# Two of eight pairs of contraction tiles in gate and up as seven products of mixed tiles in place of eight

## Chip, cores and metric

One core of a Trainium2 chip. The metric is device time in microseconds (us) of one execution, as a median of runs; the kernel before took 2430.54 us (three runs, 2429.72 to 2430.84). Durations inside the kernel come from one profiled execution.

## What is computed

A two-layer decoder trunk in fp32 over 256 tokens of width 2048: a Mamba-2 layer, then a layer of sliding-window attention, each followed by a dense SwiGLU feed-forward block, with RMSNorm around every part. The change touches the feed-forward block of both layers only:

```
D_MODEL = 2048
SEQ = 256
D_FF = -(-8 * D_MODEL // (3 * 256)) * 256      # 5632

def swiglu(u, w_gate, w_up, w_down):
    return (jax.nn.silu(u @ w_gate) * (u @ w_up)) @ w_down

for layer in range(DEPTH):
    ...
    ffn = swiglu(rmsnorm(h, g[2]), ffn_w_gate[layer], ffn_w_up[layer], ffn_w_down[layer])
    h = h + rmsnorm(ffn, g[3])
```

## The kernel before

**Tiles.** The tokens lie transposed, 16 contraction tiles (kt) of 128 features by 256 tokens; the 256 tokens are two token tiles (t) of 128. The 5632 hidden columns are worked in 11 units of 512 (`u`). In a unit, gate runs over the 16 contraction tiles for both token tiles (`a_form`, L277), then up does. The products accumulate in PSUM, one bank of 128 x 512 for each token tile; there are eight banks in all (L154).

**Three products for one.** Every fp32 number is held as a sum of a high and a low part of type fp32r. A product of two numbers is three matmuls (`a_mm`, L291): high by high, high by low, low by high (L298, L299, L300). So one token tile, one contraction tile and 512 columns cost three matmuls, and a pair of contraction tiles of gate and up for both token tiles costs 2 x 2 x 2 x 3 = 24.

**Weights.** The class `Weights` (L33) holds a list of weight tiles in the order in which they are used. A tile is two contraction tiles by 512 columns, 512 KB, loaded by SP into one of five `raw` buffers (`_load`, L54). It is then split by `_convert` (L62): ScalarE copies it to `whi` (L78), VectorE subtracts `whi` from it into `wlo` (L79); of each there are four buffers. `next` (L85) is called when TensorE's products of a tile are written down: it lets conversion run up to three tiles ahead and loads up to four ahead of that. So a tile can be converted when the tile four places earlier has had its last product, and a raw buffer can be loaded again when the tile in it is converted.

**A unit's end.** When gate is complete, ScalarE takes the Silu of both banks into `scr` (L576). When up is complete, VectorE multiplies the two banks by the row factor `rs` and by the Silu (L579). Two weight tiles into the next unit, `store` (L558) transposes the result by TensorE (eight transposes of 128 x 128, L563) and splits it into `hh` and `hl` (L186, L187), which are the input of the down products (`mix_stage`, L425). Such late steps are put on a list `todo` and called by a hook after each weight tile.

**Unit 0** differs: its gate products are interleaved with the norm and the transposes that make the tokens' tiles `xx` (`a_first`, L484).

Each engine works its instructions in the order in which they were put down; SP's queue issues the loads in the order of the list.

Of the kernel before, what the change touches and what calls it, by code (L numbers as in the profile page):

```python
# [22 lines left out]
KF = FF // P  # L23
EPS = 1e-6
NH = 64
CW = 512
HW = CW // 2
SUB = 2
RAWB = 5
CVB = 4  # L30


class Weights:  # L33

    def __init__(self, nc, pool, specs, scaled, raw_ahead=RAWB - 1, cv_ahead=CVB - 1):
        self.nc, self.pool, self.specs, self.scaled = nc, pool, specs, scaled
        self.raw_ahead, self.cv_ahead = raw_ahead, cv_ahead  # L40
        self.subs, self.first = [], {}
        for i, (key, ap) in enumerate(specs):
            a = ap.shape[1]
            n = ap.shape[2]
            per = (SUB * CW) // n
            for s in range(0, a, per):
                self.first.setdefault(key, len(self.subs))
                self.subs.append((i, s, per, n, key))
        self.raw = []
        self.cv = []  # L50
        self.pin = lambda ins: ins
        self.pos = 0

    def _load(self, upto):  # L54
        while len(self.raw) < min(upto, len(self.specs)):
            key, ap = self.specs[len(self.raw)]
            _, a, n = ap.shape
            t = self.pool.tile([P, a, n], F32, tag="raw", name="raw", bufs=RAWB)
            self.nc.sync.dma_start(t[:], ap)
            self.raw.append(t)  # L60

    def _convert(self, upto):  # L62
        nc = self.nc
        while len(self.cv) < min(upto, len(self.subs)):
            i, s, per, n, key = self.subs[len(self.cv)]
            self._load(i + 1)
            src = self.raw[i][:, s : s + per, :]
            hi = self.pool.tile([P, per, n], F32R, tag="whi", name="whi", bufs=CVB)
            lo = self.pool.tile([P, per, n], F32R, tag="wlo", name="wlo", bufs=CVB)
            if key in self.scaled:  # L70
                k0 = per * (len(self.cv) - self.first[key])
                for k in range(per):
                    f = self.scaled[key][:, k0 + k : k0 + k + 1]
                    nc.scalar.activation(hi[:, k, :], src[:, k, :], AF.Copy, scale=f)
                    nc.vector.scalar_tensor_tensor(lo[:, k, :], src[:, k, :], f, hi[:, k, :].bitcast(F32),
                                                   ALU.mult, ALU.subtract)
            else:
                self.pin(nc.scalar.copy(hi[:], src))  # L78
                self.pin(nc.vector.tensor_tensor(lo[:], src, hi[:].bitcast(F32), ALU.subtract))  # L79
            self.cv.append((hi, lo))  # L80
# [18 lines left out]
def tile_yoco(ctx: ExitStack, tc: tile.TileContext, a: dict):  # L99
    nc = tc.nc  # L100
# [9 lines left out]
    scaled = {}  # L110

    def add(key, w, kts, n0, nn=CW):
        nk = SUB * CW // nn
        for k in range(0, kts, nk):
            specs.append((key, wap(w, k, nk, n0, nn)))
# [18 lines left out]
        add("wout%d" % c, a["ssm_w_out"][0], DI // P, CW * c)  # L134

    def add_ffn(l):
        for u in range(FF // CW):
            add("gate%d_%d" % (l, u), a["ffn_w_gate"][l], KD, CW * u)
            add("up%d_%d" % (l, u), a["ffn_w_up"][l], KD, CW * u)
        for c in range(4):  # L140
            add("down%d_%d" % (l, c), a["ffn_w_down"][l], KF, CW * c)

# [37 lines left out]
    def new_xt(pool=xtpool):  # L180

        xx = pool.tile([P, KD, 2, T], F32R, tag="xx", name="xx")
        return xx[:, :, 0, :], xx[:, :, 1, :], xx

    def split_bank(dh, dl, src):
        nc.scalar.copy(dh, src)  # L186
        nc.vector.tensor_tensor(dl, src, dh.bitcast(F32), ALU.subtract)  # L187
# [116 lines left out]
    xt = new_xt()  # L304
# [99 lines left out]
    first = (xr, rr0, first_unit, first_squares, first_rstd, first_row, renorm)  # L404
# [119 lines left out]
    def row_factor():  # L524

        return [norm_stats(hpool, h, t) for t in range(NT)]
# [12 lines left out]
    def by_row(o, src, rr):  # L539

        nc.vector.tensor_tensor(o.rearrange("p (c t) -> p c t", c=2), src.rearrange("p (c t) -> p c t", c=2),
                                rr[:].unsqueeze(1).broadcast_to([P, 2, T]), ALU.mult)

    def ffn(layer, mix):
        xt = new_xt()
        with tc.tile_pool(name="ffn%d" % layer, bufs=1, side="right") as fp:
            hh = fp.tile([P, KF, T], F32R, tag="hh", name="hh")
            hl = fp.tile([P, KF, T], F32R, tag="hl", name="hl")
            scr = hpool.tile([P, 2 * NT, CW], F32, tag="gpost", name="scr")
            todo = []  # L550

            def hook():
                if todo:
                    f = todo.pop(0)
                    if f is not None:
                        f()

            def store(u):  # L558

                for t in range(NT):  # L560
                    pt = bank()
                    for k in range(4):
                        nc.tensor.transpose(pt[:, P * k : P * (k + 1)], scr[:, NT + t, P * k : P * (k + 1)], ident[:])  # L563
                    split_bank(hh[:, 4 * u : 4 * u + 4, P * t : P * (t + 1)],
                               hl[:, 4 * u : 4 * u + 4, P * t : P * (t + 1)],
                               pt[:].rearrange("p (k t) -> p k t", k=4))

            rs = None
            for u in range(FF // CW):
                if u == 0:  # L570
                    gb = a_first("gate%d_%d" % (layer, u), mix, gt[:, layer, 2, :], xt)
                    rs = row_factor()
                else:
                    gb = a_form("gate%d_%d" % (layer, u), xt, KD, hook=hook)
                for t in range(NT):
                    nc.scalar.activation(scr[:, t, :], gb[t][:], AF.Silu, scale=rs[t][:, 0:1])  # L576
                ub = a_form("up%d_%d" % (layer, u), xt, KD, hook=hook)
                for t in range(NT):
                    nc.vector.scalar_tensor_tensor(scr[:, NT + t, :], ub[t][:], rs[t][:, 0:1], scr[:, t, :],  # L579
                                                   ALU.mult, ALU.mult)  # L580
                todo += [None, lambda u=u: store(u)]
            return mix_stage("down%d_" % layer, (hh, hl), KF, layer, 3, hook=hook, lag=2 if layer == 0 else CVB)


    mix = mix_stage("wout", (yh, yl), DI // P, 0, 1, bk0=bk0)
# [497 lines left out]
```

## Time and profile before

| what | value |
|---|---|
| median of three runs | 2430.54 us |
| the profiled execution | 2430.55 us, span 2428.8 us |
| granted TensorE clock | 0.999 |
| TensorE busy | 2409.6 us, 99% of the span, 11810 matmuls |
| VectorE busy | 1461.5 us, 60% |
| ScalarE busy | 1221.8 us, 50% |
| matmuls of gate, up and the shared k and v by a_mm, each of L298, L299, L300 | 1440 |
| HBM read | 449.56 MB, 186 GB/s over the span |

The profile gives for every engine the time in which it was busy, for every group of instructions a count and a mean length, and for idle time the instruction that ended it. TensorE's matmuls overlap each other in the pipeline, so their lengths (about 390 ns) are not what one costs: the distance from start to start is. For VectorE and ScalarE the length of a group's instruction is near its cost, a little over it where one follows another.

Loads of 512 KB are issued on SP's queue, and the profile gives the time from issue to landing.

### The profile page before, as it was taken

How to read it: one execution, taken by the hardware profiler on the slowest of the kernel's cores; microseconds unless marked ns; L12 is line 12 of the kernel's file. 1: busy time of each engine (PE TensorE's matmuls, PEld its weight loads, DVE VectorE, ACT ScalarE, POOL GpSimd, SP SyncE). 2: the span in 40 equal slices, each digit the busy share in tenths (PEclk: the TensorE clock that was granted, in tenths of full speed). 3: DMA queues.
4: the chain of work that ended last, by engine and by line, in shares of the span. 5: the costliest groups of instructions: out<-in, count | busy, mean ns of one | idle time of the engine just before them, and what ended most of it. 6: DMA issues, size and time to landing. Idle time of an engine off the chain costs nothing.

```text
span 2428.8 us, 30963 instructions
## 1 busy us (share of the span) xinstructions
PE 2409.6 (99%) x11810; PEld 2001.9 (82%) x11810; DVE 1461.5 (60%) x2017; ACT 1221.8 (50%) x1721; POOL 84.2 (3%) x66
## 2 busy tenths in 40 slices
PE   9999999999999999999999999999999999999998
PEld 8888888888878888888888878777888888888887
DVE  6998878874465445445444468866545455454444
ACT  6566866654454444444444467755444444444443
POOL 2500100000000000000000000000000000000000
PEclk9999999999999999999999999999999999999999
DMA  7666666657656666666666664345666666666664
GB/s 221 183 204 190 189 189 187 178 183 249 191 169 193 185 191 191 189 190 191 205 192 194 194 187 156 127 127 154 204 190 187 191 191 190 190 190 207 193 193 145
DMA packets 284404, 453.75 MB, mean 187 GB/s; under 512 B 16976, under 2 KB 115536, under 8 KB 283488
## 3 DMA queue, kind: packets, MB, share of 16 engines
q1 hardware_dynamic: 283936, 451.39, 62.1%
q8 instruction: 92, 1.51, 0.3%
q14 instruction: 56, 0.46, 0.1%
q10 hardware_dynamic: 288, 0.33, 0.0%
q0 software_dynamic: 32, 0.07, 0.0%
HBM read 449.56 MB, written 2.16 MB: 186 GB/s over the span
## 4 chain that ended last, share of the span: by engine, by line
PE 97%; ACT 1%; DVE 1%; issue 0%; POOL 0%; DVEq 0%; POOLq 0%; ACTq 0%
PE bank L299 23%; PE bank L300 23%; PE bank L298 23%; PE bank L240 14%; PE bank L245 7%; PE bank L563 1%; PE bank L785 1%; PE bank L961 1%; PE bank L1004 1%; PE bank L360 1%; ACT xx L219 0%; PE bank L996 0%; ACT whi L78 0%; ACT junk L202 0%; PE bank L770 0%; PE bank L788 0%
## 5 line engine op out<-in xcount | busy, mean ns | idle before, releaser
L79 DVE TENSOR_TENSOR wlo<-raw,whi 128x1024 fp32r<-128x1024 f32 x785 | 960.0, 1224 | 867.0 <-ACT whi L78 866.5
L78 ACT CAST whi<-raw 128x1024 fp32r<-128x1024 f32 x785 | 826.4, 1053 | 997.3 <-PE bank L300 911.4
L298 PE MATMUL bank<-whi,xx 128*128 128x512 f32 x1440 | 562.7, 391 | 2.5 <-ACT xx L219 2.1
L300 PE MATMUL bank<-whi,xx 128*128 128x512 f32 x1440 | 561.3, 390 | 0.9 <-DVE xx L220 0.9
L299 PE MATMUL bank<-wlo,xx 128*128 128x512 f32 x1440 | 561.1, 390 | 0.5 <-DVE wlo L79 0.5
L240 PE MATMUL bank<-xx,whi 128*128 128x512 f32 (+1 forms) x1488 | 523.9, 397 | 0.0
L245 PE MATMUL bank<-xx,wlo 128*128 128x256 f32 (+1 forms) x1488 | 416.7, 285 | 0.0
L240 PEld LDWEIGHTS bank<-xx,whi 128*128 128x128 f32 (+1 forms) x1488 | 277.0, 188 | 61.2 <-issue 0.4
L298 PEld LDWEIGHTS bank<-whi,xx 128*128 128x128 f32 x1440 | 270.4, 188 | 60.2 <-ACT xx L219 4.2
L300 PEld LDWEIGHTS bank<-whi,xx 128*128 128x128 f32 x1440 | 270.4, 188 | 58.9 <-DVE xx L220 2.8
L299 PEld LDWEIGHTS bank<-wlo,xx 128*128 128x128 f32 x1440 | 270.5, 188 | 56.3 <-DVE wlo L79 1.4
L245 PEld LDWEIGHTS bank<-xx,wlo 128*128 128x128 f32 (+1 forms) x1488 | 280.5, 189 | 11.3 <-issue 7.0
L298 PE MATMUL bank<-whi,hh 128*128 128x512 f32 x704 | 274.2, 389 | 0.0
L300 PE MATMUL bank<-whi,hl 128*128 128x512 f32 x704 | 274.1, 389 | 0.0
L299 PE MATMUL bank<-wlo,hh 128*128 128x512 f32 x704 | 274.0, 389 | 0.0
L300 PEld LDWEIGHTS bank<-whi,hl 128*128 128x128 f32 x704 | 132.2, 188 | 27.5
L299 PEld LDWEIGHTS bank<-wlo,hh 128*128 128x128 f32 x704 | 132.2, 188 | 27.4
L298 PEld LDWEIGHTS bank<-whi,hh 128*128 128x128 f32 x704 | 132.2, 188 | 27.1
L298 PE MATMUL bank<-whi,yh 128*128 128x512 f32 x256 | 100.1, 391 | 0.0
L300 PE MATMUL bank<-whi,yl 128*128 128x512 f32 x256 | 99.8, 390 | 0.0
L299 PE MATMUL bank<-wlo,yh 128*128 128x512 f32 x256 | 99.7, 389 | 0.0
L194 POOL TENSOR_TENSOR rs<-ms,neghalf 128x1 f32<-128x1 f32 x8 | 4.4, 544 | 1816.5 <-DVE ms L192 1816.5
(183 smaller groups left out, 1790.9 us busy)
## 6 DMA issues: line engine op xcount, KB each, us to landing
raw<-in_ffn_w_gate_dram SPq DMA_DIRECT2D x176, 512.0 KB, 4.3
raw<-in_ffn_w_up_dram SPq DMA_DIRECT2D x176, 512.0 KB, 3.7
raw<-in_ffn_w_down_dram SPq DMA_DIRECT2D x176, 512.0 KB, 4.9
raw<-in_ssm_w_in_dram SPq DMA_DIRECT2D x161, 512.0 KB, 4.5
raw<-in_ssm_w_out_dram SPq DMA_DIRECT2D x64, 512.0 KB, 4.7
raw<-in_attn_w_q_dram SPq DMA_DIRECT2D x32, 512.0 KB, 3.4
raw<-in_attn_w_o_dram SPq DMA_DIRECT2D x32, 512.0 KB, 4.3
crow<-cumd SPq DMA_DIRECT2D x32, 256.0 KB, 3.9
```

Of the source, the lines that this page charges most:

```text
L78: self.pin(nc.scalar.copy(hi[:], src))
L79: self.pin(nc.vector.tensor_tensor(lo[:], src, hi[:].bitcast(F32), ALU.subtract))
L240: nc.tensor.matmul(o, wh, xx[:, kt, :, :].rearrange("p a t -> p (a t)"), start=(kt == 0), stop=(kt == kts - 1))
L245: nc.tensor.matmul(o[:, :T], wl, xx[:, kt, 0, :], start=False, stop=False)
L298: nc.tensor.matmul(o, sh, wh, start=(kt == 0), stop=False)
L299: nc.tensor.matmul(o, sh, wl, start=False, stop=False)
L300: nc.tensor.matmul(o, sl, wh, start=False, stop=(kt == kts - 1))
L360: nc.tensor.matmul(o[:], hi[:, kk, cs], xr[2][:, kt, :, :].rearrange("p a t -> p (a t)"), start=(kt == 0), stop=(kt == KD - 1))
L563: nc.tensor.transpose(pt[:, P * k : P * (k + 1)], scr[:, NT + t, P * k : P * (k + 1)], ident[:])
L785: nc.tensor.matmul(o[64 * q : 64 * q + 64, c0 : c0 + T], xdt[0][:, 2 * h2 + q, :], m[:, q, 0:T], start=True, stop=False)
L961: nc.tensor.matmul(pss[q][:, c0:c1], qt[pr, i, (0 if c0 == 0 else P) : (P if c0 == 0 else T)], kd[pr, j, 0:kn], start=True, stop=True)
L1004: nc.tensor.matmul(ob[64 * q : 64 * q + 64, c0 : c0 + T], v[:, 0, vs], pt[:, q, 0:T], start=True, stop=False)
```

## The change

In units 1 to 8 of each layer (`S_FIRST`, `S_LAST`), two of the eight pairs of contraction tiles are worked as seven products in place of eight. For a pair with the even tile e and the odd tile o, the gate and up products of both token tiles are a 2 x 2 by 2 x 2 block product: rows are the token tiles 0 and 1, the inner index is e and o, columns are gate and up. Strassen's scheme in Winograd's form computes it with seven block products p1 to p7 of mixed tiles:

- Token tiles (`mixed_x`, once a layer for each of the two pairs): f1 = e1 - o1, f3 = e0 - e1, f2 = e0 - f1, f0 = o0 - f2, where e0 is contraction tile e of token tile 0. VectorE makes them from `xh` and `xl`, and they are split into high and low again, in `sx`.
- Weight tiles (`_mixed`, for every unit): the raw tile a holds gate of e and up of o, b holds gate of o and up of e, each loaded as two halves of 256 KB. t13 = (gate e + up e, up e + up o), t24 = (gate e + up e + up o, that + gate o). They are made by VectorE (L87, L90, L91 of the changed kernel), and a, t13, t24 and g (the gate half of b) are converted as four weight tiles, the last one half as large. Before, the pair had two whole ones.
- Products: a gives p1 (tokens e0) and p3 (f0); t13 gives p5 (f1) and p7 (f3); t24 gives p6 (f2) and p4 (o1); g gives p2 (o0). Each is three matmuls.

The pairs are worked in the order mixed, plain, mixed, then five plain (`S_ORDER`); a plain pair is a gate tile and an up tile as before, and adds to p2, p4 (gate of token tile 0 and 1), p3 and up1 (up). After the second mixed pair p1, p5, p6 and p7 are complete and are combined by one copy of ScalarE and four sums of VectorE (L699 to L703). At the unit's end four more sums (L708) add the combinations to p2, p4, p3 and up1, and then follow Silu (L710) and the product with the row factor (L712). All eight banks are used. The two halves of `store` of the unit before come after the pairs at positions 5 and 6 (`store_half`). Because the mixed tiles need room, `hh` and `hl` are divided into the parts of units 0 to 7 and of units 8 to 10, and the second part takes the room of the mixed tiles after unit 8.

The core of the diff:

```diff
+SPAIRS = 2
+S_FIRST, S_LAST = 1, 8
 class Weights:
+            if isinstance(ap, tuple):
+                t = self.pool.tile([P, 2, CW], F32, tag="raw", name="raw", bufs=RAWB)
+                for k in range(2):
+                    self.nc.sync.dma_start(t[:, k : k + 1, :], ap[1 + k])
...
+    def _mixed(self, i, part):
+        nc, add = self.nc, ALU.add
+        ta, tb = self.raw[i - 1], self.raw[i]
+        if part == "a":
+            return ta[:]
+        if part == "g":
+            return tb[:, 0:1, :]
+        if part == "13":
+            self.t13 = self.spool.tile([P, 2, CW], F32, tag="t13", name="t13")
+            nc.vector.tensor_tensor(self.t13[:], ta[:], tb[:, 1:2, :].broadcast_to([P, 2, CW]), add)
+            return self.t13[:]
+        t24 = self.spool.tile([P, 2, CW], F32, tag="t24", name="t24")
+        nc.vector.tensor_tensor(t24[:, 0, :], self.t13[:, 0, :], ta[:, 1, :], add)
+        nc.vector.tensor_tensor(t24[:, 1, :], t24[:, 0, :], tb[:, 0, :], add)
+        return t24[:]
...
+            def mixed_x(i):
+                y = sp.tile([P, 2, T], F32, tag="sy", name="sy")
+                ks = slice(SUB * i, SUB * i + 2)
+                nc.vector.tensor_tensor(y[:], xh[:, ks, :].bitcast(F32), xl[:, ks, :].bitcast(F32), ALU.add)
+                e0, e1, o0, o1 = y[:, 0, :P], y[:, 0, P:], y[:, 1, :P], y[:, 1, P:]
+                f = sp.tile([P, 4, P], F32, tag="sf", name="sf")
+                for n, p, q in ((1, e1, o1), (3, e0, e1), (2, e0, f[:, 1, :]), (0, o0, f[:, 2, :])):
+                    nc.vector.tensor_tensor(f[:, n, :], p, q, ALU.subtract)
+                split_bank(sx[:, i, :, 0, :], sx[:, i, :, 1, :], f[:])
...
+            def mixed_unit(u):
...
+                for pos, i in enumerate(S_ORDER):
+                    e, o = SUB * i, SUB * i + 1
+                    if i < SPAIRS:
+                        for part, prods in (("a", (("p1", raw_x(e, 0)), ("p3", form(i, 0)))),
+                                            ("13", (("p5", form(i, 1)), ("p7", form(i, 3)))),
+                                            ("24", (("p6", form(i, 2)), ("p4", raw_x(o, 1)))),
+                                            ("g", (("p2", raw_x(o, 0)),))):
+                            hi, lo, _, _ = W.next("s" + key + part)
+                            for n, (name, (sh, sl)) in enumerate(prods):
+                                mm(name, sh, sl, hi[:, n, :], lo[:, n, :])
+                    else:
+                        for w, names in (("gate", ("p2", "p4")), ("up", ("p3", "up1"))):
+                            hi, lo, _, _ = W.next(w + key)
+                            for n in range(SUB):
+                                for t in range(NT):
+                                    mm(names[t], *raw_x(e + n, t), hi[:, n, :], lo[:, n, :])
+                    if pos == S_END:
+                        nc.scalar.copy(scr[:, 0, :], bk["p1"][:])
+                        nc.vector.tensor_tensor(vh[:, 0, :], bk["p6"][:], scr[:, 0, :], ALU.subtract)
+                        nc.vector.tensor_tensor(scr[:, 1, :], bk["p7"][:], vh[:, 0, :], ALU.subtract)
+                        nc.vector.tensor_tensor(vh[:, 0, :], bk["p5"][:], vh[:, 0, :], ALU.add)
+                        nc.vector.tensor_tensor(vh[:, 1, :], vh[:, 0, :], bk["p7"][:], ALU.subtract)
+                    if pos in (5, 6):
+                        store_half(u - 1, pos - 5)
+                outs = [("p2", scr[:, 0, :]), ("p4", scr[:, 1, :]), ("p3", vh[:, 0, :]), ("up1", vh[:, 1, :])]
+                for name, part in outs:
+                    nc.vector.tensor_tensor(part, bk[name][:], part, ALU.add)
```

**Where the instructions stand.** VectorE before, from the end of one unit (layer 0) into the next: the last subtractions of a unit's up tiles (the tiles are in order of use), the unit's two products with the row factor, and the next unit's first tiles with the two splits of the transposed result.

```order
L79 TENSOR_TENSOR wlo_7499<-raw_7478,whi_7498 128x1024 [waits DMAHW1_49,Activation_49]
L79 TENSOR_TENSOR wlo_7517<-raw_7496,whi_7516 128x1024 [waits DMAHW2_49,Activation_49]
L579 SCALAR_TENSOR_TENSOR scr_6477<-bank_7386,rs_6748,scr_6477 128x512 [waits PE_49]
L579 SCALAR_TENSOR_TENSOR scr_6477<-bank_7387,rs_6762,scr_6477 128x512 [waits PE_49]
L79 TENSOR_TENSOR wlo_7539<-raw_7514,whi_7538 128x1024 [waits DMAHW3_49,Activation_49]
L79 TENSOR_TENSOR wlo_7557<-raw_7536,whi_7556 128x1024 [waits DMAHW4_49,Activation_49]
L79 TENSOR_TENSOR wlo_7589<-raw_7554,whi_7588 128x1024 [waits DMAHW5_49,Activation_49]
L187 TENSOR_TENSOR hl_6476<-bank_7572,hh_6475 128x4x128 [waits Activation_49]
L187 TENSOR_TENSOR hl_6476<-bank_7579,hh_6475 128x4x128 [waits Activation_49]
```

VectorE in the changed kernel at the same kind of place, between unit 1 and unit 2 of layer 0. The banks 6990, 6982, 6958 and 7026 are p2, p4, p3 and up1 of unit 1. Raw tiles 7197 and 7216 are a and b of unit 2's first mixed pair, 7291 and 7294 of its second; 7242 is the gate tile between.

```order
L115 TENSOR_TENSOR wlo_7247<-t13_7244,whi_7246 128x1024 [waits Activation_49]
L238 TENSOR_TENSOR hl_6476<-bank_7235,hh_6475 128x4x128 [waits Activation_49]
L708 TENSOR_TENSOR scr_6482<-bank_6990,scr_6482 128x512 [waits PE_49]
L708 TENSOR_TENSOR scr_6482<-bank_6982,scr_6482 128x512 [waits PE_49]
L87 TENSOR_TENSOR t13_7343<-raw_7291,raw_7294 128x1024 [waits DMAHW3_49,DMAHW5_49,DMAHW2_49,DVE_49]
L115 TENSOR_TENSOR wlo_7268<-t24_7264,whi_7267 128x1024 [waits Activation_49]
L708 TENSOR_TENSOR vh_6481<-bank_6958,vh_6481 128x512 [waits PE_49]
L708 TENSOR_TENSOR vh_6481<-bank_7026,vh_6481 128x512 [waits PE_49]
L712 SCALAR_TENSOR_TENSOR scr_6482<-vh_6481,rs_6753,scr_6482 128x512 [waits DVE_49,Activation_49]
L712 SCALAR_TENSOR_TENSOR scr_6482<-vh_6481,rs_6767,scr_6482 128x512 [waits DVE_49,Activation_49]
L115 TENSOR_TENSOR wlo_7298<-raw_7216,whi_7297 128x512 [waits Activation_49]
L115 TENSOR_TENSOR wlo_7310<-raw_7242,whi_7309 128x1024 [waits DMAHW0_49,Activation_49]
```

Between the subtraction of the first pair's t13 and that of the next gate tile there now stand eight instructions that are no subtraction of a weight tile, among them t13 of the second pair, which waits for the loads of that pair.

SP's queue in the changed kernel at the same place, in the order of the list (raw 7172 is the last up tile of unit 1, 7341 the gate tile after unit 2's second mixed pair):

```order
L74 DMA raw_7172<-in_ffn_w_up_dram 128x2x512 [waits DMAHW6_49,DVE_49]
L70 DMA raw_7197<-in_ffn_w_gate_dram 128x512 [waits DMAHW7_49,DVE_49]
L70 DMA raw_7197<-in_ffn_w_up_dram 128x512
L70 DMA raw_7216<-in_ffn_w_gate_dram 128x512 [waits DMAHW0_49,DVE_49]
L70 DMA raw_7216<-in_ffn_w_up_dram 128x512
L74 DMA raw_7242<-in_ffn_w_gate_dram 128x2x512 [waits DMAHW1_49,DVE_49]
L74 DMA raw_7262<-in_ffn_w_up_dram 128x2x512 [waits DMAHW2_49,DVE_49]
L70 DMA raw_7291<-in_ffn_w_gate_dram 128x512 [waits DMAHW3_49,DVE_49]
L70 DMA raw_7291<-in_ffn_w_up_dram 128x512
L70 DMA raw_7294<-in_ffn_w_gate_dram 128x512 [waits DMAHW5_49,DMAHW4_49,DVE_49]
L70 DMA raw_7294<-in_ffn_w_up_dram 128x512
L74 DMA raw_7341<-in_ffn_w_gate_dram 128x2x512 [waits DMAHW7_49,DMAHW6_49,DVE_49]
```

The bytes are the same; a mixed pair has four loads in place of two. With five raw buffers, 7294 takes the buffer of 7197, five tiles earlier.

More of the change, by code (lines that the diff above doesn't have):

```diff
@@ L558, in store, with store_half @@
+            def store_half(u, t):
+                pt = bank()
+                for k in range(4):
+                    nc.tensor.transpose(pt[:, P * k : P * (k + 1)], scr[:, NT + t, P * k : P * (k + 1)], ident[:])
+                ts = slice(P * t, P * (t + 1))
+                split_bank(hid[0].at(4 * u, 4 * u + 4, ts), hid[1].at(4 * u, 4 * u + 4, ts),
+                           pt[:].rearrange("p (k t) -> p k t", k=4))
             def store(u):
                 for t in range(NT):
-                    pt = bank()
@@ L568, in ffn @@
             rs = None
             for u in range(FF // CW):
+                if S_FIRST <= u <= S_LAST:
+                    if u == S_FIRST:
+                        hid = [Cat(4 * LATE, e, None) for e in early]
+                    mixed_unit(u)
+                    if u == S_LAST:
+                        spool.__exit__(None, None, None)
+                        lpool = tc.tile_pool(name="late%d" % layer, bufs=1, side="right")
+                        lp = lpool.__enter__()
+                        for n, hx in enumerate(hid):
+                            hx.tiles = (early[n], lp.tile([P, KF - 4 * LATE, T], F32R, tag="late%d" % n, name="late"))
+                        todo += [None, lambda u=u: store(u)]
+                    continue
```

93 lines of the change are left out of this document (78 added, 15 removed).

## The prediction

> **What bounds the kernel now.** I read the page's busy shares first, then the chain that ended last, then one feed-forward unit by windows.
>
> ```profile
> PE 2409.6 (99%) x11810; PEld 2001.9 (82%) x11810; DVE 1461.5 (60%) x2017; ACT 1221.8 (50%) x1721; POOL 84.2 (3%) x66
> PE 97%; ACT 1%; DVE 1%; issue 0%; POOL 0%; DVEq 0%; POOLq 0%; ACTq 0%
> 1000.00:1044.41 44.41, 44.41 (x201) 36.88 (x201) 22.12 (x21) 19.10 (x20) 0.00 (x0) 1.00 0.66 190
> ```
>
> The chain is 97% TensorE, so the time is the length of TensorE's instruction stream, and only two things can move it: products leaving the stream, and gaps entering it. The third row is one whole unit of gate and up (columns: length, then busy time of PE, weight load, DVE, ACT, POOL, then clock, DMA share, GB/s). TensorE is busy for all 44.41 us at full clock; VectorE works 22.12 of them, ScalarE 19.10. Those are the reserves that the change draws on.
>
> ```profile
> 1003.22 0.39 PE L300 MATMUL bank<-whi,xx 128*128 128x512 f32 x1
> 1003.65 1.05 ACT L78 CAST whi<-raw 128x1024 fp32r<-128x1024 f32 x1 [1.67 <-PE bank L300]
> 1004.74 1.23 DVE L79 TENSOR_TENSOR wlo<-raw,whi 128x1024 fp32r<-128x1024 f32 x1 [1.50 <-ACT whi L78]
> ...
> 1006.37 1.05 ACT L78 CAST whi<-raw 128x1024 fp32r<-128x1024 f32 x1 [1.67 <-PE bank L300]
> ```
>
> This is the rhythm of a weight tile. Its cast starts when the tile four back has had its last product (3.22 + 0.39 = 3.61, cast at 3.65), the subtraction follows the cast (3.65 + 1.05, starts at 4.74) and the next cast comes 2.72 us later. Twelve products fit into 2.72 us, so **one product is 0.2267 us** of stream; 192 of them are 43.5 us of the 44.41. A consumer starts 0.43 us after the start of the last product it waits for, which is 0.20 after the next product's start.
>
> **The change part by part.**
>
> *Products removed.* A mixed pair has 21 products (seven, three each) in place of 24; two pairs a unit, 8 units a layer, 2 layers: 96 products, 96 x 0.2267 = **21.8 us less**.
>
> The Trainium skill, "TensorE: Matmul & The Clock Gate", section "Back-to-back issue gap", gives about 131 ns per 512-wide product in a sustained stream with weight loads. By that figure the 96 would be worth 12.6 us. The trace disagrees with 0.2267 us, so I keep 21.8.
>
> *Transposes split.* The eight transposes of a unit's result stood together; now four stand after each of two weight tiles.
>
> ```profile
> 1014.33 1.03 PE L563 MATMUL bank<-ident,scr 128*128 128x128 f32 x8
> ...
> 1015.12 0.48 PE L298 MATMUL bank<-whi,xx 128*128 128x512 f32 x1
> 1015.44 0.40 PE L299 MATMUL bank<-wlo,xx 128*128 128x512 f32 x1
> ```
>
> The eight take 0.79 us from start to start (about 0.1 each), and the first product behind them is followed after 0.32 instead of 0.23: 0.09 us per block. A second block costs 0.09 more; 16 units: **+1.5 us** (ends: nothing, and double).
>
> *VectorE's added work.* Per unit it has 18 whole subtractions and 2 halves (before: 16 whole), two sums of 1024 (t13), four of 512 (t24), four sums out of PSUM after the second pair, four at the unit's end, and the old two products with the row factor and two splits.
>
> ```profile
> L79 DVE TENSOR_TENSOR wlo<-raw,whi 128x1024 fp32r<-128x1024 f32 x785 | 960.0, 1224 | 867.0 <-ACT whi L78 866.5
> L579 DVE SCALAR_TENSOR_TENSOR scr<-bank,rs,scr 128x512 f32<-128x512 f32 x44 | 30.9, 743 | 0.0
> L187 DVE TENSOR_TENSOR hl<-bank,hh 128x512 fp32r<-128x512 f32 x44 | 28.2, 683 | 0.0
> L438 DVE TENSOR_TENSOR bank<-bank,gpost 128x512 f32<-128x512 f32 x32 | 22.0, 697 | 7.2 <-ACT junk L435 5.1 <-ACT whi L78 2.1
> L399 DVE TENSOR_TENSOR y<-xx 128x1024 f32<-128x1024 f32 x4 | 4.8, 1212 | 0.0
> L541 DVE TENSOR_TENSOR qt<-qt,rr 128x512 f32<-128x512 f32 x8 | 5.5, 688 | 0.1
> ```
>
> With 1.224 for a subtraction, 1.212 for a sum of two 1024-wide tiles, 0.69 for any 512-wide one and 0.743 for a product with the factor: 22.0 + 1.4 + 2.4 + 2.8 + 2.8 + 2.8 + 1.5 + 1.4 = 37 us in a unit of about 43. It fits on the whole; whether it fits in place decides. The added work stands in the first 15 us of the unit, and a weight tile can be prepared only three tiles ahead.
>
> *The tight place.* VectorE works its queue in order, so I add up the queue at a unit's start (the rows of the order in the section on the change), with 0 where TensorE's stream reaches the mixed unit's first product. First, how close VectorE's instructions follow one another:
>
> ```profile
> 1007.46 1.23 DVE L79 TENSOR_TENSOR wlo<-raw,whi 128x1024 fp32r<-128x1024 f32 x1 [1.50 <-ACT whi L78]
> 1008.60 1.40 DVE L579 SCALAR_TENSOR_TENSOR scr<-bank,rs,scr 128x512 f32<-128x512 f32 x2
> 1016.75 1.28 DVE L187 TENSOR_TENSOR hl<-bank,hh 128x512 fp32r<-128x512 f32 x2
> ```
>
> The second starts 1.14 after the first, though that lasts 1.23; two of 0.743 fill 1.40 and two of 0.683 fill 1.28. So independent ones cost 1.14, 0.66 and 0.60 in a row, 0.09 less than they last. The queue then reads:
> - The tile of gate's last pair ends at -2.72. The sums out of p2 and p4 can start 0.20 later: -2.52 and -1.92.
> - t13 of the second pair at -1.32, if its raw tiles have landed.
> - Subtraction of the first pair's t24 at -0.18, done at 1.04. TensorE wants it at 2.72: 1.7 us to spare.
> - Sums out of p3 and up1 at 0.96 and 1.56 (allowed from 0.20), products with the factor at 2.16 and 2.82.
> - Subtraction of the first pair's last half tile (g) at 3.47, done at 4.15. TensorE wants it at 4.31, its second product: 0.16 to spare, of which 0.05 go for the handover (estimate from the 0.04 above).
> - Subtraction of the next gate tile at 4.07, done at 5.29, seen at 5.34. TensorE has run 21 products and two more of this tile by 5.21: it **stops for 0.13 us**.
> - After that VectorE gains: the second pair's t24 is cast by 11.1 and subtracted by 12.4, wanted from 13.2.
>
> So 0.13 us a unit, in the 14 units that follow a mixed one (the first of each layer has two fewer sums ahead of it): **+1.8 us**. Nothing else shortens that wait; ends: 0, and the case "full lengths" below.
>
> *ScalarE.* It has 18 whole and 2 half casts, one copy and four older instructions, about 23 us; whole casts take 1.05.
>
> ```profile
> L186 ACT CAST hh<-bank 128x512 fp32r<-128x512 f32 x44 | 23.5, 586 | 0.0
> ```
>
> The casts of t24 and g at the unit's start end near -1.5 and 0.8 by the same adding up, ahead of VectorE. Nothing.
>
> *Loads.* A pair is now four loads of 256 KB in place of two of 512 KB, four more a unit for SP at 0.37 each, which stand in SP's waiting time.
>
> ```profile
> SPq L59 <- DVE wlo L79: 74.2, 32, 3.2
> L59 SPq DMA_DIRECT2D raw<-in_ffn_w_gate_dram x16: 367/368/368, 961.6 to 1047.7; - x16
> DMA to landing us min/median/max: 3.5/4.0/4.7
> out_dram<-h SPq DMA_DIRECT2D x7, 256.0 KB, 2.6
> gpost<-in_norm_w_dram SPq DMA_DIRECT2D x4, 1024.0 KB, 7.6
> h<-in_x_dram SPq DMA_DIRECT2D x2, 1024.0 KB, 8.7
> ```
>
> What matters is one tile: the second pair's b (gate of the odd, up of the even tile). Of five raw buffers it takes the one of the first pair's a, which is free when a's subtraction ends. Going back through the queue: the gate tile whose buffers a's cast takes ends at -8.65 (three tiles of 2.72 and half the transposes, 0.49, lie between it and 0), so the cast runs from -8.45 to -7.40, its subtraction to -6.14. The two halves of b are issued at -6.1 and -5.7. With 3.5 to 4.7 for 512 KB they land at -2.6 to -1.0; 4.0 after the second issue is **-1.7, needed at -1.32**. I take it as on time. The ends: a 256 KB load alone took 2.6, and if b counts as the second half of one stream of 1 MB begun with the tile before it (issued at -8.5), 7.6 to 8.7 give -0.9 to +0.2, up to 1.5 late.
>
> *Mixed tokens.* At each layer's start VectorE makes the token differences: one 512-wide sum, four of 128 and a split per pair, some 5 us a layer.
>
> ```profile
> 720.59 1.23 DVE L79 TENSOR_TENSOR wlo<-raw,whi 128x1024 fp32r<-128x1024 f32 x1 [2.85 <-ACT whi L78]
> ```
>
> They stand among the subtractions of up of unit 0, where VectorE waits 2.85 us and then over half its time. Nothing; without that cover at most 5 us a layer.
>
> *PSUM.* All eight banks are in use in a mixed unit; p7, p6 and p2 of a unit wait for VectorE's four sums. The last of these ends at 2.2, p6 is wanted at 2.72. Nothing, while the queue above holds.
>
> *Sum.* -21.8 + 1.5 + 1.8 = -18.5 us. The profiled execution took 2430.55 us (span 2428.8, so 1.75 around it), the same as the median of 2430.54: **2412.0 us**.
>
> **The rivals.**
> - *No stop at all.* The four sums run a little shorter or TensorE's transposes cost nothing more: 2430.5 - 21.8 = 2408.7. For it: 0.13 us is smaller than what the adding up can resolve. Against: it has nothing in hand either.
> - *b a little late.* t13 waits for the load, and all behind it moves; every us late is a us of stop, 16 units. At the slowest landing of the trace (-1.0) it is 0.3 us: 2412 + 5 = 2417. For it: the margin is 0.4 us against a spread of 1.2.
> - *Full lengths.* If VectorE's instructions followed one another by their whole lengths, nine steps of 0.09 would add 0.8 us a unit: 14 x 0.8 = 11, 2423. Against: the starts above. The Trainium skill has such a rule: "VectorE: DVE Perf Modes", section "Terms", says that after each instruction the pipe drains before the next can issue. The starts 1.14 apart at a length of 1.23 show that here it doesn't lengthen the row, but the new sums read PSUM and what the last one wrote.
> - *The pair's loads on the path: slower.* Place: t13 of the second pair, at the head of VectorE's queue. If b lands 1.5 us late (the 1 MB bound), each unit stops for 1.6 and saves 1.26: 16 x 0.4, about 2436. It decides from b landing 1.1 us after it is needed (1.26 less 0.13), 5.5 us after the second half's issue. Against: 512 KB loads under the same traffic took at most 4.7.
>
> **How the numbers follow.** Chances: forecast (2410 to 2414.5) 0.58, no stop (2408.5 to 2410) 0.12, b a little late (2414.5 to 2421) 0.15, full lengths (to 2425) 0.05, loads on the path 0.10, half of it within 0.2% and half slower. 0.2%, 4.9 us, is about what a measurement here tells from no change. The range takes in the first two cases and most of the third: 2408.5 to 2419. Faster 0.90, same 0.05, slower 0.05.
>
> **What would show it.** A mixed unit should span about 43.3 us (44.41 before), with 186 products; VectorE busy about 36 us of it. The waits of TensorE should name the subtraction of the first gate tile after the first pair, 0.1 to 0.2 us each. If t13 shows idle time behind a load, the third or fourth rival holds, and its size says which. If p7, p6 or p2 wait for the sums, the queue was longer than added up. Products spaced other than 0.2267 us would break the first term.

## The result, and the profile after

| | median us | runs |
|---|---|---|
| before | 2430.69 | 2429.72 to 2431.09 (4) |
| changed | 2411.24 | 2410.53 to 2411.84 (4) |
| ratio | 0.9921 | 95% interval 0.9909 to 0.9933 |

The changed kernel is 19.45 us faster; 18.5 were predicted. The profiled executions say the same: spans of 2428.8 and 2409.7, 19.1 apart. First the page of the changed kernel: its first line, the busy shares, and the chain that ended last.

```profile
span 2409.7 us, 31424 instructions
PE 2390.0 (99%) x11714; PEld 1980.7 (82%) x11714; DVE 1667.9 (69%) x2329; ACT 1279.7 (53%) x1805; POOL 87.2 (4%) x66
PE 97%; ACT 1%; DVE 1%; issue 0%; POOL 0%; DVEq 0%; POOLq 0%; ACTq 0%
```

TensorE has 96 matmuls fewer and still holds 97% of the chain. VectorE went from 60% to 69% busy: 206 us of added work that the chain hardly shows.

A unit's length is read from a fixed landmark, the first transposes of a unit's result, from one unit to the next. These are their groups in units 1 and 2 of the changed kernel (unit 1 is the first mixed one), and those of two neighbouring units before (name, count, length in ns, first and last start).

```profile
L644 PE MATMUL bank<-ident,scr x4: 270/272/273, 773.7 to 774.0; 128*128 128x128 f32 x4
L644 PE MATMUL bank<-ident,scr x4: 270/272/272, 816.9 to 817.2; 128*128 128x128 f32 x4
...
L563 PE MATMUL bank<-ident,scr x8: 270/272/273, 1014.3 to 1015.1; 128*128 128x128 f32 x8
L563 PE MATMUL bank<-ident,scr x8: 270/272/273, 1058.7 to 1059.5; 128*128 128x128 f32 x8
```

816.9 - 773.7 = 43.2, and 1058.7 - 1014.3 = 44.4. With the starts to a hundredth the pair shown is 43.18 apart; most units take **43.15 or 43.16 after, and 44.41 before**, 1.25 less. Six products of 0.2267 are 1.36, so 0.11 came back: the second block of transposes (0.09 predicted) and no stop. That is the rival "no stop at all" in most units, and yet the total came out near the forecast. Where the rest went shows at four other units, below.

One whole mixed unit by windows (length; busy time of PE, weight load, DVE, ACT, POOL; clock, DMA share, GB/s):

```profile
785.54:828.71 43.17, 43.17 (x195) 35.69 (x194) 34.52 (x39) 22.59 (x25) 0.00 (x0) 1.00 0.62 196
```

TensorE has no idle time in it. VectorE works 34.5 of 43.2 us, against 22.1 of 44.4 before.

Now the tight place: VectorE's timeline at the start of that unit, whose first mixed product stands at 785.54 (start, length, engine, line, what).

```profile
782.08 0.68 DVE L238 TENSOR_TENSOR hl<-bank,hh 128x512 fp32r<-128x512 f32 x1
782.68 1.28 DVE L708 TENSOR_TENSOR scr<-bank,scr 128x512 f32<-128x512 f32 x2
783.88 1.22 DVE L87 TENSOR_TENSOR t<-raw 128x1024 f32<-128x1024 f32 x1
785.01 1.22 DVE L115 TENSOR_TENSOR wlo<-t,whi 128x1024 fp32r<-128x1024 f32 x1
786.15 1.28 DVE L708 TENSOR_TENSOR vh<-bank,vh 128x512 f32<-128x512 f32 x2
787.35 1.41 DVE L712 SCALAR_TENSOR_TENSOR scr<-vh,rs,scr 128x512 f32<-128x512 f32 x2
788.67 4.09 DVE L115 TENSOR_TENSOR wlo<-raw,whi 128x512 fp32r<-128x512 f32 x4
```

Nothing here waits: each starts 0.08 or 0.09 before the one ahead has ended. The last row begins with the half tile g at 788.67; the gate tile follows 0.60 later, at 789.27, and is done at 790.49. TensorE at the same place:

```profile
790.08 0.39 PE L673 MATMUL bank<-whi,xx 128*128 128x512 f32 x1
790.30 0.62 PE L671 MATMUL bank<-whi,xx 128*128 128x512 f32 x2
790.76 0.40 PE L672 MATMUL bank<-wlo,xx 128*128 128x512 f32 x1
```

The tile's first matmul that reads `wlo` stands at 790.76, 0.27 after the subtraction's end and on TensorE's own 0.23 spacing. With some 0.05 for the handover, about 0.2 us is to spare. Note the second row: two matmuls that need only `whi` stand ahead of the first that needs `wlo`, which is not the order in which `mm` writes them. The program's builder plans each engine's order anew, so that the engines work in the order of the built program and not of the written one. This mattered in the experiments.

The first mixed unit of the layer looks otherwise. VectorE's t13 of the first pair, SP's two halves of the second pair's b, VectorE's t13 of that pair, then TensorE at the same plain gate tile (in brackets the idle time ahead and what ended it); the first product of unit 1 stands at 741.90.

```profile
730.25 1.23 DVE L87 TENSOR_TENSOR t<-raw 128x1024 f32<-128x1024 f32 x1 [2.12 <-DMA raw<-in_ffn_w_up_dram]
...
736.28 0.33 SPq L70 DMA_DIRECT2D raw<-in_ffn_w_gate_dram  x1
736.66 0.42 SPq L70 DMA_DIRECT2D raw<-in_ffn_w_up_dram  x1
...
741.17 1.23 DVE L87 TENSOR_TENSOR t<-raw 128x1024 f32<-128x1024 f32 x1 [2.16 <-DMA raw<-in_ffn_w_up_dram]
...
746.66 0.39 PE L671 MATMUL bank<-whi,xx 128*128 128x512 f32 x1
747.25 0.50 PE L672 MATMUL bank<-wlo,xx 128*128 128x512 f32 x1 [0.20 <-DVE wlo L115]
747.58 0.39 PE L673 MATMUL bank<-whi,xx 128*128 128x512 f32 x1
```

Here b came late: t13 started 4.5 us after the second half's issue, having waited 2.16 us, and TensorE's matmul at 747.25 starts 0.59 after the one before instead of 0.23. The one behind it costs 0.33. That is 0.36 + 0.10 us. In layer 1 the same place shows a gap from 1730.76 to 1731.30, 0.42 us in all.

A late b is not a matter of the first unit alone. These are rows of unit 2 of layer 1, whose first product stands at 1769.58: SP's second half of b, VectorE's t13, and how long the two halves took to land.

```profile
1763.85 0.42 SPq L70 DMA_DIRECT2D raw<-in_ffn_w_up_dram  x1
1768.37 1.23 DVE L87 TENSOR_TENSOR t<-raw 128x1024 f32<-128x1024 f32 x1 [0.37 <-DVE scr L708]
...
DMA to landing us min/median/max: 2.7/3.6/4.4
```

The bracket names the sum just ahead, but that had ended 0.36 us before; the second half landed 4.4 us after its issue, at 1768.29, and t13 started then. It was issued 5.73 us ahead of the unit's first product, exactly as in unit 2 of layer 0, where the same half took 3.3 us. This unit is 0.37 us longer than the others (43.52), and unit 4 of layer 1, in which t13 started 0.10 us behind the end of the sum ahead, 0.12 (43.27). So of the 16 units' 20.0 us (16 x 1.25) about 1.4 went again in four units, which leaves 18.6. The span is 19.1 shorter; the other 0.5 isn't found in these units, and no run puts it down to the change.

### The profile page after: what moved, and what is told of

Same layout as the page of the kernel before. It is cut to its first block, busy times and chain, and to the rows that moved or that the text cites. A ratio compares the mean times of both kernels' runs of the same rounds, so it can differ in the third digit from the quotient of the medians.

```text
span 2409.7 us, 31424 instructions
## 1 busy us (share of the span) xinstructions
PE 2390.0 (99%) x11714; PEld 1980.7 (82%) x11714; DVE 1667.9 (69%) x2329; ACT 1279.7 (53%) x1805; POOL 87.2 (4%) x66
## 3 DMA queue, kind: packets, MB, share of 16 engines
HBM read 449.56 MB, written 2.16 MB: 187 GB/s over the span
## 4 chain that ended last, share of the span: by engine, by line
PE 97%; ACT 1%; DVE 1%; issue 0%; POOL 0%; DVEq 0%; POOLq 0%; ACTq 0%
PE bank L291 14%; PE bank L350 14%; PE bank L351 14%; PE bank L349 14%; PE bank L672 9%; PE bank L673 9%; PE bank L671 9%; PE bank L296 7%; PE bank L644 1%; PE bank L949 1%; PE bank L1125 1%; PE bank L1168 1%; DVE wlo L115 1%; PE bank L411 1%; ACT xx L270 0%; PE bank L1160 0%
## 5 line engine op out<-in xcount | busy, mean ns | idle before, releaser
L115 DVE TENSOR_TENSOR wlo<-raw,whi 128x1024 fp32r<-128x1024 f32 (+1 forms) x785 | 936.1, 1200 | 568.8 <-ACT whi L114 567.6
L114 ACT CAST whi<-raw 128x1024 fp32r<-128x1024 f32 (+1 forms) x785 | 811.1, 1036 | 828.9 <-PE bank L351 506.3
L672 PE MATMUL bank<-wlo,xx 128*128 128x512 f32 x864 | 336.9, 390 | 0.3 <-DVE wlo L115 0.2
L671 PE MATMUL bank<-whi,xx 128*128 128x512 f32 x864 | 337.2, 393 | 0.0
L673 PE MATMUL bank<-whi,xx 128*128 128x512 f32 x864 | 336.9, 390 | 0.0
L349 PE MATMUL bank<-whi,hh 128*128 128x512 f32 x512 | 199.3, 389 | 0.0
L351 PE MATMUL bank<-whi,hl 128*128 128x512 f32 x512 | 199.2, 389 | 0.0
L350 PE MATMUL bank<-wlo,hh 128*128 128x512 f32 x512 | 199.2, 389 | 0.0
L672 PEld LDWEIGHTS bank<-wlo,xx 128*128 128x128 f32 x864 | 162.3, 188 | 35.2 <-DVE wlo L115 2.1
L673 PEld LDWEIGHTS bank<-whi,xx 128*128 128x128 f32 x864 | 162.2, 188 | 34.2
L671 PEld LDWEIGHTS bank<-whi,xx 128*128 128x128 f32 x864 | 162.2, 188 | 32.8
L349 PE MATMUL bank<-whi,xx 128*128 128x512 f32 x416 | 162.6, 393 | 2.5 <-ACT xx L270 2.1
L351 PE MATMUL bank<-whi,xx 128*128 128x512 f32 x416 | 162.5, 392 | 0.9 <-DVE xx L271 0.9
L350 PE MATMUL bank<-wlo,xx 128*128 128x512 f32 x416 | 162.3, 391 | 0.5 <-DVE wlo L115 0.5
L114 ACT CAST whi<-t 128x1024 fp32r<-128x1024 f32 x64 | 67.2, 1050 | 107.7 <-DVE t L91 49.8
```

The lines of the kernel that those rows point to most:

```text
L349: nc.tensor.matmul(o, sh, wh, start=(kt == 0), stop=False)
L350: nc.tensor.matmul(o, sh, wl, start=False, stop=False)
L351: nc.tensor.matmul(o, sl, wh, start=False, stop=(kt == kts - 1))
L671: nc.tensor.matmul(o, sh, wh, start=(n == 1), stop=False)
L672: nc.tensor.matmul(o, sh, wl, start=False, stop=False)
L673: nc.tensor.matmul(o, sl, wh, start=False, stop=(n == total[name]))
```

## The experiments

Ratios are against the kernel before on the same chip.

| run | edit | median us | ratio, 95% interval |
|---|---|---|---|
| e1_drop6 | before, six matmuls a unit left out | 2409.11 | 0.9912, 0.9897 to 0.9928 |
| e2_prod24 | changed, p2's matmuls twice | 2431.84 | 1.0005, 0.9995 to 1.0015 |
| e3_spairs3 | changed, three mixed pairs | 2418.48 | 0.995, 0.9935 to 0.9966 |
| e4_sum_tight | changed, one more sum in the tight place | 2411.56 | 0.9918, 0.9896 to 0.9939 |
| e5_pin | changed, matmuls kept in written order | 2413.72 | 0.993, 0.9915 to 0.9945 |
| e6_pin_sum | e5 and e4 together | 2422.22 | 0.9965, 0.9952 to 0.9978 |
| e7_b_twice | changed, b loaded twice | 2411.47 | 0.9919, 0.9903 to 0.9936 |
| e8_spread3 | three pairs, further apart, `store` whole | 2401.73 | 0.988, 0.9865 to 0.9895 |
| e9_together | changed, `store` whole | 2410.99 | 0.992, 0.9905 to 0.9935 |
| e10_spread4 | four pairs, each followed by a plain one | 2430.95 | 1.0003, 0.9993 to 1.0013 |

**What a product is worth, and what the mixing costs (e1, e2).** In e1 the kernel before, otherwise untouched, loses as many matmuls as the change removes:

```diff
+ less = key.startswith("up") and 1 <= int(key.split("_")[1]) <= 8 and k0 + kk in (1, 5)
- a_mm(bk, xh, xl, hi, lo, kk, k0 + kk, kts, n0, nn)
+ a_mm(bk, xh, xl, hi, lo, kk, k0 + kk, kts, n0, nn, ts=range(NT - less))
```

> The kernel before with six matmuls left out in up of each of the units 1 to 8 of both layers (contraction tiles 1 and 5, token tile 1), and nothing else changed: 96 matmuls fewer, no mixing. It computes less than the reference. Theory (a matmul is worth 0.2267 us of TensorE's stream, and nothing else decides): 2430.6 - 21.8 = 2408.9 us. Rival (a matmul in a sustained stream is worth 0.131 us): 2418.

e2 puts them back into the changed kernel:

```diff
+ if name == "p2":
+     for x_, w_ in ((sh, hi), (sh, lo), (sl, hi)):
+         nc.tensor.matmul(bk[name][:], x_, w_[:, n, :], start=False, stop=False)
```

> The changed kernel with three more matmuls for each mixed pair (p2's three repeated, so that its output is not the reference's): 24 in place of 21, with all mixing kept. Theory (the gain is the matmul count alone, the mixing costs 2 to 3 us): 2411.2 + 21.8 = 2433, some 2 us above the kernel before. Rival (the mixed order also shortens the stream in another way, or the stops at the unit's start are worth more than 1 us in all and the extra matmuls cover them): 2430 or less.

e1 is 21.9 us below the kernel before (2431.05 on that chip): 0.228 us for each of 96. Its shortened units take 43.05, 1.36 less than 44.41, which is six times 0.2267. The Trainium skill, "TensorE: Matmul & The Clock Gate", section "Back-to-back issue gap", has about 131 ns for a 512-wide product in a sustained stream with weight loads; estimated by that figure e1 would stand 12.6 us below, at about 2418, and the measurement decides for 0.2267. With the count of products restored, e2 is 0.8 us above before, with an interval of about -1.2 to +3.6 that includes no change: **the mixing itself is nearly free**. Its units take 44.49 where the old ones take 44.41; the 0.08 fits the second block of transposes. The stops of the first units have almost gone in it: TensorE's weight loads wait 1.0 us in all for these `wlo`, 2.1 in the changed kernel. One stop is left in a later unit, the third of layer 1, which is 0.69 longer (45.18), with t13 waiting 0.90 us for b. The three added matmuls stand right ahead of the plain gate tile and give VectorE 0.68 us more, which fits with a time below the 2433 expected.

**How much the tight place has in hand (e3, e4).** e3 sets one number:

```diff
-SPAIRS = 2
+SPAIRS = 3
```

> Three mixed pairs of eight in place of two. Theory (matmul count, VectorE's queue recovers after the second pair and has room at the third): 48 matmuls fewer, 2411.2 - 10.9 = 2400.3 us, no new waits of TensorE. Rival (VectorE, at some 41 of 42.5 us a unit by whole lengths, is full): it stops TensorE 0.5 to 1 us a unit, 2408 to 2416.

The theory was wrong by 18 us. Timelines of e3 at the plain gate tile after the second pair, VectorE, then TensorE:

```profile
843.13 1.23 DVE L87 TENSOR_TENSOR t<-raw 128x1024 f32<-128x1024 f32 x1 [0.88 <-DMA raw<-in_ffn_w_up_dram]
844.27 2.35 DVE L115 TENSOR_TENSOR wlo<-raw,whi 128x1024 fp32r<-128x1024 f32 x2
...
844.42 0.39 PE L671 MATMUL bank<-whi,xx 128*128 128x512 f32 x1
845.54 0.50 PE L672 MATMUL bank<-wlo,xx 128*128 128x512 f32 x1 [0.73 <-DVE wlo L115]
```

The third pair's t13 stands ahead of the gate tile's subtraction and waits 0.88 us for its load; its first subtraction ends at 845.49, and TensorE stops. In all of e3 the matmuls of this line waited 8.9 us for `wlo` and their weight loads 25.6, against 0.2 and 2.1 in the changed kernel. It is not this t13 alone: those of the second pairs wait too, 0.3 to 0.8 us in all but one of the units from the second on. So a third pair in the same rhythm turns its 10.9 us (48 x 0.2267) into a loss of 7.2 against two pairs. That the pairs stand too near to one another is an argument so far; e8 moves them apart.

e4 adds one sum of 512 whose result nobody reads, right behind the four at the unit's end:

```diff
+ dm = sp.tile([P, CW], F32, tag="dm", name="dm")
...
+ nc.vector.tensor_tensor(dm[:], vh[:, 0, :], vh[:, 1, :], ALU.add)
```

> The changed kernel with one more sum of 512 on VectorE at each mixed unit's end, behind the four sums out of PSUM and ahead of the subtraction of the half tile g. Theory (the queue at the unit's start has 0.2 us to spare and passes on what is over): 0.60 - 0.22 = 0.38 us in each of 14 units, 2411.2 + 5.3 = 2416.5. Rival (VectorE has room there, only its total counts): 2411.2.

Nothing happened to the time. Yet the sum is there, as these rows of VectorE, then of TensorE, of e4 show. The unit's first product stands at 785.84 here, 0.30 later than above.

```profile
788.31 0.68 DVE L710 TENSOR_TENSOR dm<-vh 128x512 f32<-128x512 f32 x1
789.58 4.09 DVE L115 TENSOR_TENSOR wlo<-raw,whi 128x512 fp32r<-128x512 f32 x4
...
789.92 0.84 PE L672 MATMUL bank<-whi,xx 128*128 128x512 f32 x3
790.60 0.39 PE L673 MATMUL bank<-wlo,xx 128*128 128x512 f32 x1
```

g's subtraction, at 789.58, stands 0.91 later than in the changed kernel, so 0.61 later in its unit. The row "x3" shows what took that up: in e4 the builder put three matmuls that need only `whi` side by side, ahead of the late `wlo`. The written program was changed in one place and the built one in two. In the units with b on time the run tells nothing of the queue. In two others b was late, and there it shows its price: in units 2 and 4 of layer 1 t13 waited 0.95 and 0.56 us for the load, and these units are 0.93 and 0.53 us longer than the rest (44.06 and 43.66 against 43.13).

**The same with the order held (e5, e6).** In e5 the matmuls of the mixed units keep the order in which they are written; e6 has e4's sum as well.

```diff
- nc.tensor.matmul(o, sh, wh, start=(n == 1), stop=False)
+ pin(nc.tensor.matmul(o, sh, wh, start=(n == 1), stop=False))
```

(and likewise for the other two)

> The changed kernel with the matmuls of the mixed units held to the order in which they are written (high by high, high by low, low by high of each product), so that none with a cast tile alone is drawn ahead of a late subtraction. Both theories: the subtraction of the first gate tile is done at 4.95 us into the unit by the trace of the changed kernel and wanted at 4.99; no stop to speak of, 2411 to 2412 us.

> e5 with the one more sum of 512 of e4 in VectorE's queue at the unit's end. Theory (the queue is tight, and in e4 the order of TensorE's matmuls hid the sum): the half tile g is late by 0.15 and the gate tile by 0.47 us more, 0.6 in each of 14 units: e5 + 8.7, about 2420. Rival (VectorE has room there): as e5.

Most of e5's units take 43.29 to 43.33, 0.15 more than the changed kernel's: 2.4 us over 16 units, as the medians have it (2.5), though their intervals overlap. One `whi` matmul drawn ahead gives the changed kernel 0.23 us of slack, and pinned it has none. e6 is 8.5 us above e5, its intervals well apart, and most of its units take 43.89. TensorE in e6:

```profile
834.33 0.39 PE L672 MATMUL bank<-whi,xx 128*128 128x512 f32 x1
834.73 0.50 PE L673 MATMUL bank<-wlo,xx 128*128 128x512 f32 x1
835.07 0.40 PE L674 MATMUL bank<-whi,xx 128*128 128x512 f32 x1
835.30 0.39 PE L672 MATMUL bank<-whi,xx 128*128 128x512 f32 x1
835.86 0.50 PE L673 MATMUL bank<-wlo,xx 128*128 128x512 f32 x1 [0.17 <-DVE wlo L115]
```

Two distances, 0.40 and 0.56 in place of 0.23, at g and at the gate tile, each with 0.11 more behind it. One VectorE instruction of 0.60 us costs 0.58 us a unit when TensorE can't step around it. **The queue was tight as the prediction had it**; the changed kernel lives on a margin of a few tenths.

**The load of b (e7).** Each half of b is loaded twice, so that it lands later:

```diff
- for k in range(2):
+ for k in range(2) if ap[0] == "a" else (0, 1, 0, 1):
```

> The changed kernel with each tile b loaded twice over (512 KB more for a pair, the same data). Theory (the second pair's t13 waits for b, with about 0.2 us to spare): b lands some 2.2 us later, TensorE stops for up to 2 us in each of 16 units: 2430 to 2446, about the time of the kernel before or above it. Rival (loads are hidden in any case): 2411 to 2412.

Again no change, and again for a reason in the order. VectorE of e7 near the start of the same unit, after the factor products:

```profile
789.61 3.00 DVE L115 TENSOR_TENSOR wlo<-raw,whi 128x512 fp32r<-128x512 f32 x3
792.53 1.22 DVE L87 TENSOR_TENSOR t<-raw 128x1024 f32<-128x1024 f32 x1
```

The second pair's t13 now stands behind the subtractions of g and of the plain gate and up tiles, at 792.53; in the changed kernel it stands at 783.88, ahead of the four sums' second half. Moved there, it waits for nothing. The run shows that a later b costs nothing where t13 can move; it doesn't test the rival "loads on the path" with t13 in its old place. What that costs is seen without this run, in the units of layer 1 above: 0.37 us for a wait of 0.37 in the changed kernel, 0.93 and 0.53 for 0.95 and 0.56 in e4. A late b costs about what t13 waits, as the prediction had it. A b that is late by 1 us or more in every unit was not run.

**Room to go further (e8, e9, e10).** e8 takes three pairs, but puts two plain pairs ahead of the third, and `store` whole, behind all mixing:

```diff
+SPAIRS = 3
+    S_ORDER = [0, 3, 1, 4, 5, 2, 6, 7]
-                    if pos in (5, 6):
-                        store_half(u - 1, pos - 5)
+                    if pos == 6:
+                        store(u - 1)
```

> Three mixed pairs as in e3, but at positions 0, 2 and 5 in place of 0, 2 and 4, and the transposes of the unit before together behind position 6. Theory (the stops of e3 come from the third pair's t13 and its wait for a load ahead of the plain gate tile, while VectorE still works off the second pair; VectorE as a whole is not full): the stops of 1.1 us a unit shrink to a few tenths, 2400 to 2404. Rival (VectorE's total is the limit with three pairs): 2414 or more, as e3.

The windows of one of its units:

```profile
785.00:827.45 42.45, 42.45 (x193) 35.11 (x192) 38.57 (x44) 24.21 (x28) 0.00 (x0) 1.00 0.61 199
```

42.45 is 183 products of 0.2267 (41.49), one block of transposes with what follows it (0.88) and 0.08 us besides. The third pair costs 7 us with one plain pair ahead of it and gains 9.5 with two (some 1.3 of it through the whole `store`, by the 0.08 a unit of e9 below): **2401.73 us, 28.9 below the kernel before, 9.5 below the change**. VectorE is now busy for 38.6 of 42.5 us.

This isn't the distance between the pairs alone. The builder gave e8 another order as well, as VectorE's rows at the start of the same unit show:

```profile
788.60 4.09 DVE L115 TENSOR_TENSOR wlo<-raw,whi 128x512 fp32r<-128x512 f32 x4
792.61 1.22 DVE L87 TENSOR_TENSOR t<-raw 128x1024 f32<-128x1024 f32 x1
```

As in e7, the second pair's t13 stands behind the subtractions and waits for nothing, where e3 has it ahead of them (784.62, after a wait of 0.40). How much of the gain is the order's and how much the distance's, no run separates.

e9 keeps two pairs and puts `store` whole at position 5, to price the split transposes by themselves:

```diff
-                    if pos in (5, 6):
-                        store_half(u - 1, pos - 5)
+                    if pos == 5:
+                        store(u - 1)
```

> The changed kernel with the eight transposes of the unit before in one block behind position 5, as the kernel before had them. Theory (a second block of transposes costs 0.09 us of TensorE's stream): 16 x 0.09 less, 2411.2 - 1.4 = 2409.8 us, and 0.09 us less in a unit's length by the trace. Rival (the blocks cost nothing, or one block puts ScalarE's and VectorE's splits in the way of the tight place): 2411.2 or above.

Most of its units take 43.08, which is 0.08 less, as the 0.09 had it. The total, 0.25 less than the changed kernel's, can't be told from no change: weight loads for the plain tiles waited for `wlo` 15 times for 3.5 us in all, against 5 times for 2.1. The unit that has the late b in the changed kernel lost 0.92 here (44.00), with t13 waiting 0.76.

e10 takes four pairs, each followed by a plain one (`S_ORDER = [0, 4, 1, 5, 2, 6, 3, 7]`, `store` whole at position 7, the tiles of `mixed_x` in the buffers of t24 and t13 for room).

> Four mixed pairs of eight, at positions 0, 2, 4 and 6, the transposes of the unit before behind position 7. Theory (VectorE's total now is the limit): with three spread pairs VectorE is busy about 39.1 of 43 us; a fourth adds 1.5 subtractions (1.7 us), t13 (1.1) and t24 (1.2), 43.2 us, over the 41.8 that TensorE's stream would take; a unit takes 43.2 or more, 2414 or above, slower than three. Rival (the saving of matmuls goes on): 2401.7 - 10.9 = 2390.8.

All of the gain is gone. A window of 43 us of e10, and a matmul in it:

```profile
780.00:823.00 43.00, 41.52 (x183) 32.89 (x182) 41.10 (x47) 24.45 (x29) 0.00 (x0) 1.00 0.59 193
...
788.00 0.50 PE L671 MATMUL bank<-whi,sx 128*128 128x512 f32 x1 [0.68 <-DVE hl L238]
```

VectorE is busy for 41.10 of 43.00 us, nearly full, and a unit takes 44.1 to 45.4 us where 180 products and the transposes are 41.7. TensorE waits in turn for a subtraction, for a cast by ScalarE and, here, for the split of the transposes. That VectorE's total is the limit fits with this; no run separates it from the order of the pairs.

## Why the prediction was right

**Products removed, 21.8 predicted.** Right: 21.9 in e1.

**Transposes split, +1.5.** Right: 0.08 a unit between e2 and before, and 0.08 between e9 and the change.

**A stop of 0.13 us in 14 units, +1.8.** Mis-sized. The place and the queue were right, in their order and nearly in their steps, but all of it ran 0.34 us earlier: the sums began at -2.86 instead of -2.52, t13 at -1.66 instead of -1.32, g at 3.13 instead of 3.47. The step that failed is the first line of the queue, which let the sums out of p2 and p4 both wait for the end of gate's last tile. p2's last matmul comes three matmuls before that end, so VectorE could begin as soon as it was through with the split at 782.08. That was enough for no stop at all where b was on time, with 0.2 us in hand, as the 0.13 had been within the error of such a sum.

**b's load on time.** Right in 12 of the 14 units from unit 2 on: in unit 2 of layer 0 its halves were issued at 779.43 and 779.81 (-6.11 and -5.73; -6.1 and -5.7 predicted), and t13 didn't wait. The landing was the uncertain step: 4.0 us after the second issue were taken, and in these 14 units it was 3.0 to 4.4, the latest about 0.4 behind the need. (The 2.6 given for a lone 256 KB load belongs to a row of stores, `out_dram<-h`.) Why the load of unit 2 of layer 1 took 4.4 stays open.

In the first mixed unit of a layer b was late too: in layer 0 it was issued at -5.62 and -5.24, and the second half took 4.4 us. The issue was 0.5 later because the first pair's t13, which waits for a load in every unit, started later there: 11.65 us ahead of the first product (730.25), against 12.92 in unit 2 (772.62, after a wait of 1.85). That put off the subtraction that frees the buffer. The longer landing is the larger part: with the 3.3 us of unit 2 this b would have been there in time. The prediction took the first unit to be safer, having fewer sums ahead (four, not the two it says); that its b comes later was left out. It cost some 0.5 us in each layer.

So the stops that there were, about 1.4 us, stand in other units than the 1.8 predicted, and for the reason of the rival "b a little late". That the sum came within 0.8 us because they are nearly as large is luck. That these few tenths are the real risk of the change is shown by e6, where 0.6 us of work in the tight place is worth 8.5 us, and by e3, where a third pair with its waits for loads came out 18 us above its forecast.

**VectorE's work.** 37 us a unit were added up from lengths, 34.5 are busy: 39 instructions, most of which begin 0.09 before the one ahead has ended, and busy time counts that once. The rival "full lengths" fell by the same rows, the sums out of PSUM among them. The rule of the Trainium skill behind it ("VectorE: DVE Perf Modes", section "Terms": the pipe drains before the next instruction issues) doesn't lengthen the row here. **Mixed tokens, ScalarE, PSUM:** nothing, as predicted; e2, which has all of them, leaves 0.8 us for everything besides the products.

## What to carry to other kernels

When one engine's stream is the time, removed instructions pay their start-to-start distance, and the risk lies in one short stretch where the engine that pays for it has to fit its queue. Add up that stretch instruction by instruction, take each start from its own releaser rather than from the end of the tile, carry a load through it with the whole spread of its landing, and do it also for the first unit after a change of rhythm, not just for a steady one. An experiment that adds an instruction or a load to such a stretch tests the builder as much as the chip: hold the order, or read it again, before a result of "no change" is believed.

## What the chip showed besides

A matmul that comes late is followed after 0.33 or 0.34 us (747.25 to 747.58, 834.73 to 835.07) instead of 0.2267: a stop costs 0.1 us more than its gap, in these traces for gaps from 0.02 to 0.9 us (845.54, followed at 845.88). In e5 a handover late by 0.02 us (833.64 where 833.62 was due) cost 0.13 in this way.
